# A sigmoid gate in one ScalarE pass, row scales by Newton steps on VectorE, and another order for the last tile

## The chip, the cores and the metric

The kernel runs on one core of a Trainium2 chip. The metric is the device time of one execution in microseconds (us). The kernel before the change took 1693.11 us (median of three runs, 1692.22 to 1693.23). The engines are named as in the profile: PE is TensorE (its matmuls; PEld is its weight loads), ACT is ScalarE, DVE is VectorE, POOL is GpSimd, SP is SyncE, which here only issues DMAs.

## What is computed

One encoder layer over 1280 tokens (1024 of one request, 256 of another) of width 1024, all in f32: an input projection, two kinds of attention, an output projection, a squared-ReLU MLP, and then the part that this document is about, a gated embedding and the final norm:

```python
def _rms_norm(x, g, eps):
    xf = x.astype(jnp.float32)
    y = xf * lax.rsqrt(jnp.mean(xf * xf, axis=-1, keepdims=True) + eps)
    return (y * g.astype(jnp.float32)).astype(x.dtype)

# end of the layer
    gate = jax.nn.sigmoid(jnp.einsum('bsd,de->bse', _rms_norm(h, g_ple, NORM_EPS), w_ple_gate))
    h = h + gate * jnp.einsum('bsp,pd->bsd', p_l, w_ple_proj)
    return h
# after the only layer
    return _rms_norm(h, g_final, NORM_EPS)
```

`h` is 1280 x 1024, `w_ple_gate` is 1024 x 1024, `p_l` is 1280 x 256 and `w_ple_proj` is 256 x 1024.

## The kernel before

Tokens lie in ten tiles of 128 rows. A matrix product in near-f32 precision is made of three products of rounded parts (high times high, high times low, low times high), so that the gate of one tile and one half of the columns is 24 matmuls (8 blocks of 128 rows, three products each) of 512 columns, and the embedding's product is 6. The last stage, from about 1535 us on, is a loop over the ten tiles in the order `FORD`; before it come the last products of the MLP.

For each tile `gate_input` (L1510) transposes the tile on PE (`trg`, 8 matmuls), splits it into its high part on ACT (L1518) and its low part on DVE (L1519), and takes the sum of squares of each row on ACT in two halves (L1523, into `gss`). From that sum `rsqrt` (L135) makes the row scale `rn`: a scale and an offset on DVE (L138), a logarithm and an exponential on ACT (L139, L140), and one correction step on ACT and DVE (L142 to L144). L1527 turns its sign. `gate_input` of a tile is called one turn of the loop ahead, and its transposes stand on PE one further tile ahead.

Then `gate` (L1580) runs the 24 matmuls of a half into a PSUM bank `psg` and makes the sigmoid out of parts: an exponential on ACT (L1592), a limit and plus one on DVE (L1593), a logarithm and an exponential on ACT, which together are the reciprocal (L1594, L1595), and one correction step on POOL and DVE (L1596, L1597). `embed` (L1600) runs the 6 matmuls of the embedding into a bank `psp`. `add` (L1610) multiplies the two on DVE (L1613), subtracts the result from `h` (its sign is turned) on POOL (L1615), and takes the sum of squares of the new rows on ACT (L1616, into `fss`). For the last two tiles (`late`) POOL's two operations are made on DVE.

When both halves are done, `rsqrt` makes the row scale `rf` of the final norm, L1644 multiplies each half by `rf` and the gain `gfin` on DVE, and a DMA of 256 KB on SP's queue writes it to `y` (L1645).

The last tile is cut into three pieces of 512, 256 and 256 columns. Their three gates come first on PE, then the three embeddings. For the two small pieces the gain is multiplied in ahead of the row scale (L1634), so that ACT can finish them (L1639) while DVE finishes the first piece (L1644); the DMAs for the two halves both stand on SP's queue.

The order within each engine is made by a list scheduler from the order in which the code is written and from its own model of durations; `tc.issue_after` adds an edge by hand. All of ACT's functions here (exponential, logarithm, square, copy) are in one table set, loaded once at the start (L115).

Of the kernel before, what the change touches and what calls it, by code (L numbers as in the profile page):

```python
# [14 lines left out]
F32 = mybir.dt.float32  # L15
F32R = mybir.dt.float32r
F16 = mybir.dt.float16
AF = mybir.ActivationFunctionType
ALU = mybir.AluOpType
AX = mybir.AxisListType  # L20
# [3 lines left out]
P = 128  # L24
D = 1024
# [20 lines left out]
def encoder_kernel(ctx: ExitStack, tc: tile.TileContext, x, xT, pT, w_in, w_out, w_ff1, w_ff2, w_gate, w_proj,  # L46
# [88 lines left out]
    def rsqrt(dst, src, scale, eps, tp, n, tag):  # L135
        vv = tp.tile([P, n], F32, tag=f"{tag}v", name=f"{tag}v")
        uu = tp.tile([P, n], F32, tag=f"{tag}u", name=f"{tag}u")
        V.tensor_scalar(vv, src, scale, eps, op0=ALU.mult, op1=ALU.add)  # L138
        S.activation(uu, vv, AF.Ln)  # L139
        S.activation(dst, uu, AF.Exp, scale=-0.5)  # L140
        if n == 1:
            S.activation(uu, dst, AF.Copy, scale=-0.5)  # L142
            V.scalar_tensor_tensor(vv, dst, dst, vv, op0=ALU.mult, op1=ALU.mult)
            V.scalar_tensor_tensor(dst, vv, -3.0, uu, op0=ALU.add, op1=ALU.mult)  # L144
            return
# [3 lines left out]
        V.tensor_tensor(dst, dst, uu, op=ALU.mult)  # L149

    rstd1 = cp.tile([P, NT], F32, name="rstd1")

# [889 lines left out]
    while owed > 0:  # L1042
        d = next(side)
# [466 lines left out]
    def gate_input(t):  # L1510
# [10 lines left out]
        for n in range(2):  # L1521
            jk = gq_.tile([P, 512], F32, tag="gjk", name="gjk", bufs=1)
            S.activation(jk, h_half(t, n), AF.Square, accum_out=ss[:, n:n + 1])  # L1523
        V.tensor_tensor(ss[:, 0:1], ss[:, 0:1], ss[:, 1:2], op=ALU.add)
        rn = gq_.tile([P, 1], F32, tag="grn", name="grn")
        rsqrt(rn, ss[:, 0:1], 1.0 / D, 1e-6, gq_, 1, "grs")
        S.activation(rn, rn, AF.Copy, scale=-1.0)  # L1527
        return n3h, n3l, rn

    QUADS = {2: (0, 0, "H6"), 3: (0, 1, "L2"), 4: (1, 0, "H4"), 5: (1, 1, "L3")}  # L1530
# [27 lines left out]
    for ti, t in enumerate(FORD):  # L1558
# [16 lines left out]
            banks[0].append(pj("psg"))  # L1575
            banks[1].append(bank("tr", "psp"))

        ends = []

        def gate(i):  # L1580
            n0, nn = pieces[i]
            n = slice(n0, n0 + nn)
            ps = banks[0][i][:, :nn]
            pr = []
            for k in range(KD):
                pr += [(n3h[:, k], gw[k][0][:, n]), (n3h[:, k], gw[k][1][:, n]), (n3l[:, k], gw[k][0][:, n])]
            for m, (a, b) in enumerate(pr):
                ends[:] = [PE.matmul(ps, a, b, start=m == 0, stop=m == len(pr) - 1)]  # L1588

            e = gq_.tile([P, 512], F32, tag="ge", name="ge", bufs=3)[:, :nn]  # L1590
            d = gq_.tile([P, 512], F32, tag="gd", name="gd")[:, :nn]
            S.activation(e, ps, AF.Exp, scale=rn)  # L1592
            V.tensor_scalar(d, e, 1e18, 1.0, op0=ALU.min, op1=ALU.add)  # L1593
            S.activation(e, d, AF.Ln)  # L1594
            S.activation(e, e, AF.Exp, scale=-1.0)  # L1595
            (V if late else G).tensor_tensor(d, d, e, op=ALU.mult)  # L1596
            V.scalar_tensor_tensor(e, d, -2.0, e, op0=ALU.add, op1=ALU.mult)  # L1597
            return e

        def embed(i):  # L1600
# [9 lines left out]
        def add(i, e, pq):  # L1610
            n0, nn = pieces[i]
            n = slice(n0, n0 + nn)
            V.tensor_tensor(e, pq, e, op=ALU.mult)  # L1613
            h = h_half(t, n0 // 512)[:, n0 % 512:n0 % 512 + nn]
            (V if late else G).tensor_tensor(h, h, e, op=ALU.subtract)  # L1615
            S.activation(e, h, AF.Square, accum_out=ss[:, i:i + 1])  # L1616
# [12 lines left out]
        i = 2 if last else 1  # L1629
        V.tensor_tensor(ss[:, 0:1], ss[:, 0:1], ss[:, i:i + 1], op=ALU.add)  # L1630
        if last:

            for (n0, nn), e in zip(pieces[1:], es[1:]):
                V.tensor_tensor(e, h_half(t, 1)[:, n0 - 512:n0 - 512 + nn], gfin[:, n0:n0 + nn], op=ALU.mult)  # L1634
        rf = gq_.tile([P, 1], F32, tag="rf", name="rf", bufs=1)
        rsqrt(rf, ss[:, 0:1], 1.0 / D, 1e-6, gq_, 1, "rf")
        if last:
            for (n0, nn), e in zip(pieces[1:], es[1:]):
                S.activation(h_half(t, 1)[:, n0 - 512:n0 - 512 + nn], e, AF.Copy, scale=rf)  # L1639
            dma(y[t * P:(t + 1) * P, 512:], h_half(t, 1))  # L1640
        for n0 in range(0, 512 if last else D, 512):
            n = slice(n0, n0 + 512)
            h = h_half(t, n0 // 512)
            V.scalar_tensor_tensor(h, h, rf, gfin[:, n], op0=ALU.mult, op1=ALU.mult)  # L1644
            dma(y[t * P:(t + 1) * P, n], h)  # L1645


def _rope_tables():
# [48 lines left out]
```

## Time and profile before

| what | us |
|---|---|
| three runs, median | 1693.11 |
| the profiled execution, its own time | 1691.84 |
| its span, first to last instruction | 1690.1 |
| PE busy | 1651.6 (98% of the span) |
| DVE, ACT, POOL busy | 1179.9, 868.0, 661.0 |
| mean granted TensorE clock | 0.997 |

The page's busy times are means over the whole program. The change touches only the last tenth of it, so the views that matter are those of the stretch from 1535 us to the end. In the rows of the timeline the columns are: start in us, length in us, engine, line and operation, what is written `<-` what is read with the shape, how many instructions were merged (`x24`), and in brackets how long the engine had been idle before it and what ended that. A row of the busy-time table by stretches has the stretch, its length, and for each engine the busy time with the number of instructions, then the granted clock, the DMA share and GB/s.

### The profile page before, as it was taken

To read this page: it belongs to the slowest core of one execution; us is meant where nothing else is said; L and a number is where in the kernel's file an instruction comes from. 1 tells how busy PE (TensorE), PEld (TensorE's weight loads), DVE (VectorE), ACT (ScalarE), POOL (GpSimd) and SP (SyncE) were. 2 spreads that over 40 slices of the span, in tenths; PEclk is the share of its full clock that TensorE was granted. 3 is DMA by queue.
4 is the path that set the end of the run, shared out by engine and by line. 5 is a ranking of instruction groups with operands and counts; after the bars stand their busy time and mean duration, and the time that the engine had idled before them with its cause. 6 is when DMAs were issued, how large, how long until landed. Compare 5 with 4: busy or idle time off the path is not lost.

```text
span 1690.1 us, 27269 instructions
## 1 busy us (share of the span) xinstructions
PE 1651.6 (98%) x9849; PEld 1482.7 (88%) x9849; DVE 1179.9 (70%) x2119; ACT 868.0 (51%) x1749; POOL 661.0 (39%) x647
## 2 busy tenths in 40 slices
PE   8999999999899999999999999999999999999997
PEld 8999888888788888889999999998888888888886
DVE  7778588777888888668666666666665855445666
ACT  8643377776766667674333333233433333354554
POOL 1223455555654445433566665620532400001441
PEclk9999999999999999999999999999999999999999
DMA  9766843433954524395443343349676356532111
GB/s 309 239 216 237 247 144 110 133 108 98 273 161 130 154 74 131 108 330 172 160 136 131 132 159 128 135 169 386 220 225 203 124 192 210 177 117 75 35 44 50
DMA packets 191867, 278.28 MB, mean 165 GB/s; under 512 B 13674, under 2 KB 121076, under 8 KB 191732
## 3 DMA queue, kind: packets, MB, share of 16 engines
q1 hardware_dynamic: 189988, 271.28, 49.7%
q0 software_dynamic: 1600, 5.24, 1.0%
q8 instruction: 78, 1.28, 0.3%
q14 instruction: 57, 0.47, 0.1%
q10 hardware_dynamic: 144, 0.00, 0.0%
HBM read 182.63 MB, written 88.61 MB: 160 GB/s over the span
## 4 chain that ended last, share of the span: by engine, by line
PE 79%; DVE 8%; ACT 4%; issue 4%; POOL 2%; DMA 2%; POOLq 0%; SPq 0%; ACTq 0%; DVEq 0%
PE psa L264 6%; PE sc L651 6%; PE av L729 5%; PE psb L264 4%; PE pso L264 4%; PE tr L705 4%; PE psv L264 2%; PE psg L1588 1%; DVE pl L716 1%; DVE p L686 1%; DMA xt<-in_x 1%; POOL hq L1615 1%; DMA xr<-in_xT 1%; PE f__15605 L156 1%; PE f__16642 L156 1%
## 5 line engine op out<-in xcount | busy, mean ns | idle before, releaser
L1384 ACT ACTIVATE ao<-ar 128x1280 fp32r<-128x1280 f32 x56 | 71.2, 1273 | 183.7 <-PE f__15946 L156 36.6
L651 PE MATMUL sc<-kt,qt 128*128 128x512 f32 (+1 forms) x576 | 156.6, 392 | 8.8 <-ACT p L676 6.1
L716 DVE TENSOR_TENSOR pl<-tr,ph 128x512 fp32r<-128x512 f32 x204 | 138.0, 685 | 32.0 <-ACT ph L711 30.8
L1386 DVE TENSOR_TENSOR ao<-ar,ao 128x1280 fp32r<-128x1280 f32 x56 | 93.3, 1666 | 85.2 <-ACT ao L1384 85.2
L711 ACT ACTIVATE ph<-tr 128x512 fp32r<-128x512 f32 x204 | 120.0, 596 | 59.2 <-PE tr L705 52.7
L651 PEld LDWEIGHTS sc<-kt,qt 128*128 128x128 f32 x576 | 98.8, 189 | 27.1 <-ACT p L676 7.6
L264 PE MATMUL pso<-ow,mt 128*128 128x512 f32 x480 | 119.9, 396 | 2.0 <-DVE osq L756 1.3
L705 PE MATMUL tr<-ident,p 128*128 128x128 f32 x768 | 116.0, 274 | 5.8 <-DVE pl L716 5.1
L1588 PE MATMUL psg<-gw,n 128*128 128x512 f32 (+1 forms) x504 | 113.7, 381 | 0.0
L705 PEld LDWEIGHTS tr<-ident,p 128*128 128x128 f32 x768 | 91.6, 141 | 22.6 <-DVE pl L716 9.0
L1105 POOL TENSOR_SCALAR w1r<-w1r,gmlp 128x256 f32<-128x256 f32 x112 | 80.3, 735 | 68.4 <-DMA w1r<-in_w_ff 68.4
L1588 PEld LDWEIGHTS psg<-gw,n 128*128 128x128 f32 x504 | 90.9, 188 | 17.8
L264 PEld LDWEIGHTS pso<-ow,mt 128*128 128x128 f32 x480 | 88.0, 189 | 19.9 <-DVE osq L756 2.0
L729 PE MATMUL av<-ph,vt 128*128 128x256 f32 x544 | 101.8, 288 | 1.0 <-ACT ph L711 0.4
L690 POOL TENSOR_SCALAR p<-p,rl 128x1024 f32<-128x1024 f32 x64 | 76.2, 1192 | 50.6 <-DVE rl L688 49.1
L1178 ACT ACTIVATE w<-w1s 128x512 fp32r<-128x512 f32 x56 | 35.2, 629 | 114.7 <-POOL w1s L1185 55.3
L668 DVE TENSOR_REDUCE mm<-sc 128x1 f32<-128x1024 f32 (+1 forms) x80 | 84.2, 1056 | 9.4 <-PE sc L651 9.0
L729 PE MATMUL av<-pl,vt 128*128 128x256 f32 x408 | 89.4, 300 | 0.0
L729 PEld LDWEIGHTS av<-ph,vt 128*128 128x128 f32 x544 | 81.8, 188 | 6.4 <-DVE osq L756 0.8
L676 ACT ACTIVATE p<-sc,mm 128x1024 f32<-128x1024 f32 x64 | 71.4, 1116 | 25.1 <-DVE mm L668 16.3
L664 DVE CUSTOM_DVE_ANT_0 p<-sc,dist 128x1024 f32<-128x1024 f32 x64 | 77.6, 1218 | 7.8 <-PE sc L651 3.8
L673 ACT ACTIVATE p<-p,mm 128x1024 f32<-128x1024 f32 x64 | 73.5, 1149 | 18.0 <-DVE mm L664 17.2
(1520 smaller groups left out, 4705.9 us busy)
## 6 DMA issues: line engine op xcount, KB each, us to landing
ar<-ad SPq DMA_DIRECT2D x56, 640.0 KB, 4.0
w2r<-in_w_ff SPq DMA_DIRECT2D x56, 512.0 KB, 4.6
qt<-qd SPq DMA_DIRECT2D x160, 128.0 KB, 3.0
ad<-q SPq DMA_DIRECT2D x64, 320.0 KB, 2.8
ad<-qs SPq DMA_DIRECT2D x48, 320.0 KB, 2.2
w1r<-in_w_ff SPq DMA_DIRECT2D x28, 512.0 KB, 4.3
md<-ml SPq DMA_DIRECT2D x40, 256.0 KB, 2.5
mt<-md SPq DMA_DIRECT2D x20, 512.0 KB, 5.7
```

Of the source, the lines that this page charges most:

```text
L264: PE.matmul(ps, a, b, start=i == 0, stop=i == n - 1)
L651: PE.matmul(ps[:, h0:h0 + n], shared["q"][:, cc, v, i * P:(i + 1) * P], kt[:, s0 + h0:s0 + h0 + n], start=v == 0, stop=v == 1)
L664: V.tensor_tensor_reduce(out=p[:, :sn], in0=ps[:, :sn], in1=dst_t[:, off:off + sn], scale=SLOPES[idx], scalar=3.0e38, op0=ALU.add, op1=ALU ...
L668: V.tensor_reduce(out=st["m", i][:, 0:1], in_=ps[:, :sn], axis=AX.X, op=ALU.max, negate=True)
L690: G.tensor_scalar(p[:, :sn], p[:, :sn], rl[:, 0:1], 1.0, op0=ALU.mult, op1=ALU.mult)
L705: PE.transpose(t[:, jj, i * P:(i + 1) * P], st["ws"][i][:, j * P:(j + 1) * P], ident)
L711: S.activation(ph, st["tr", j2], AF.Copy)
L716: V.tensor_tensor(pl, st["tr", j2], f(st["ph", j2][:]), op=ALU.subtract)
L729: PE.matmul(st["av"][:, :256], x_, y_, start=j2 == 0 and n == 0, stop=j2 == nj - 1 and n == len(pr) - 1)
L1105: G.tensor_scalar(raw[:, k], raw[:, k], gmlp[:, 4 * kh + k:4 * kh + k + 1], 1.0, op0=ALU.mult, op1=ALU.mult)
L1386: V.tensor_tensor(ao[:, 1], a, f(ao[:, 0]), op=ALU.subtract)
L1588: ends[:] = [PE.matmul(ps, a, b, start=m == 0, stop=m == len(pr) - 1)]
```

## The change

Three things are edited.

The gate becomes one ACT pass, `Sigmoid` of the PSUM bank times the row scale (L1609 of the new text); the six operations that made it out of parts are gone, and the product is added to `h` and not subtracted. Sigmoid is in another table set, so a load stands ahead of the first one; the last tile loads the former set again by hand, behind its last sigmoid, for the logarithm and exponential of the final `rsqrt`.

The row scales of all tiles but the last one's final norm come from `rsqrt_d`: a first guess out of the number's bits and three Newton steps, nine small DVE operations of 128x1 in all (L158 to L165), none on ACT.

In the last tile the first piece's embedding is put ahead of the third piece's gate on PE; the sums of squares are written into a buffer of their own; the sum of the first two pieces is scaled before the third one's is there; the gain is multiplied into all three pieces ahead of the row scale; and the second half's DMA is issued on ACT's queue, while the first half's stays on SP's.

```diff
+    def rsqrt_d(dst, ss, tp, n, tag, eng=V, bufs=None, rest=None):
+        vv = tp.tile([P, n], F32, tag=f"{tag}v", name=f"{tag}v", bufs=bufs)
+        uu = tp.tile([P, n], F32, tag=f"{tag}u", name=f"{tag}u", bufs=bufs)
+        c = -0.5e-6
+        if rest is not None:
+            eng.tensor_scalar(uu, rest, -0.5 / D, c, op0=ALU.mult, op1=ALU.add)
+            c = uu
+        eng.tensor_scalar(vv, ss, -0.5 / D, c, op0=ALU.mult, op1=ALU.add)
+        eng.tensor_scalar(dst.bitcast(I32), vv[:].bitcast(I32), -0.5, float(0x5F3759DF - 2**30 - 2**22), op0=ALU.mult, op1=ALU.add)
+        for _ in range(3):
+            if n == 1:
+                eng.tensor_scalar(uu, dst, dst, vv, op0=ALU.mult, op1=ALU.mult)
+                eng.tensor_scalar(dst, uu, 1.5, dst, op0=ALU.add, op1=ALU.mult)
...
-        V.tensor_tensor(ss[:, 0:1], ss[:, 0:1], ss[:, 1:2], op=ALU.add)
         rn = gq_.tile([P, 1], F32, tag="grn", name="grn")
-        rsqrt(rn, ss[:, 0:1], 1.0 / D, 1e-6, gq_, 1, "grs")
-        S.activation(rn, rn, AF.Copy, scale=-1.0)
+        rsqrt_d(rn[:], ss[:, 1:2], gq_, 1, "grs", rest=ss[:, 0:1])
...
-            S.activation(e, ps, AF.Exp, scale=rn)
-            V.tensor_scalar(d, e, 1e18, 1.0, op0=ALU.min, op1=ALU.add)
-            S.activation(e, d, AF.Ln)
-            S.activation(e, e, AF.Exp, scale=-1.0)
-            (V if late else G).tensor_tensor(d, d, e, op=ALU.mult)
-            V.scalar_tensor_tensor(e, d, -2.0, e, op0=ALU.add, op1=ALU.mult)
+            sig[:] = [S.activation(e, ps, AF.Sigmoid, scale=rn)]
...
-            (V if late else G).tensor_tensor(h, h, e, op=ALU.subtract)
+            (V if late else G).tensor_tensor(h, h, e, op=ALU.add)
+            if last:
+                e = gq_.tile([P, 512], F32, tag="gjk", name="gjk", bufs=1)[:, :nn]
             S.activation(e, h, AF.Square, accum_out=ss[:, i:i + 1])
 
         if last:
-            es = [gate(i) for i in range(3)]
-            with tc.issue_after(ends[0].ins):
-                qs = [embed(i) for i in range(3)]
+            es = [gate(i) for i in range(2)]
             for i in range(3):
-                add(i, es[i], qs[i])
+                if i == 1:
+                    es.append(gate(2))
+                    with tc.issue_after(sig[0].ins):
+                        S.preload_act_table_set("natural_log_exp_and_others")
+                with tc.issue_after(ends[0].ins):
+                    pq = embed(i)
+                add(i, es[i], pq)
                 if i == 1:
                     V.tensor_tensor(ss[:, 0:1], ss[:, 0:1], ss[:, 1:2], op=ALU.add)
+                    V.tensor_scalar(ss[:, 0:1], ss[:, 0:1], 1.0 / D, 1e-6, op0=ALU.mult, op1=ALU.add)
...
+            premult(0)
+            first = rsqrt(rf, ss[:, 2:3], 1.0 / D, ss[:, 0:1], gq_, 1, "rf")
+            with tc.issue_after(first.ins):
+                premult(1)
+                premult(2)
+        else:
+            rsqrt_d(rf[:], ss[:, i:i + 1], gq_, 1, "rf", rest=ss[:, 0:1])
         if last:
+            V.tensor_scalar(h_half(t, 0), es[0], rf, None, op0=ALU.mult)
+            dma(y[t * P:(t + 1) * P, :512], h_half(t, 0))
             for (n0, nn), e in zip(pieces[1:], es[1:]):
                 S.activation(h_half(t, 1)[:, n0 - 512:n0 - 512 + nn], e, AF.Copy, scale=rf)
-            dma(y[t * P:(t + 1) * P, 512:], h_half(t, 1))
...
+            S.dma_start(y[t * P:(t + 1) * P, 512:], h_half(t, 1))
```

The instructions of each engine stand in the same order as before up to the last products of the MLP, among which the first row scales of the gate are made. Three places show what moves at the end of the program. The first is ACT at the end of the last tile, before (`psg` is the gate's bank, `ge` and `gd` are its scratch, `fss` the sums of squares):

```order
L1592 ACTIVATE ge<-psg,grn 128x256
L1594 ACTIVATE ge<-gd 128x256
L1595 ACTIVATE ge<-ge 128x256
L1592 ACTIVATE ge<-psg,grn 128x256
L1594 ACTIVATE ge<-gd 128x256
L1595 ACTIVATE ge<-ge 128x256
L1616 ACTIVATE ge,fss<-hq 128x512
L1616 ACTIVATE ge,fss<-hq 128x256 x2
L139 ACTIVATE rfu<-rfv 128x1
L140 ACTIVATE rf<-rfu 128x1
L142 ACTIVATE rfu<-rf 128x1
L1639 ACTIVATE hq<-ge,rf 128x256 x2
```

and with the change:

```order
L1609 ACTIVATE ge<-psg,grn 128x512
L1609 ACTIVATE ge<-psg,grn 128x256
L1630 ACTIVATE gjk,fss<-hq 128x512
L1609 ACTIVATE ge<-psg,grn 128x256
L1638 ACT_TABLE_LOAD
L1630 ACTIVATE gjk,fss<-hq 128x256 x2
L140 ACTIVATE rfu<-rfv 128x1
L141 ACTIVATE rf<-rfu 128x1
L143 ACTIVATE rfu<-rf 128x1
L1666 ACTIVATE hq<-ge,rf 128x256 x2
L1667 DMA y<-hq 128x512
```

One pass per piece is left of three, the first piece's square (L1630) now stands ahead of the last piece's sigmoid, a table load stands between that sigmoid and the last two squares, and ACT issues a DMA at its end.

The second place is DVE in the last tile (its rows before stand in the same stretch as L1593, L1596, L1597, L1613 and L1615 of three pieces, interleaved). With the change, from the first piece's product on:

```order
L1625 TENSOR_TENSOR ge<-psp,ge 128x512
L1627 TENSOR_TENSOR hq<-hq,ge 128x512
L1651 TENSOR_TENSOR ge<-hq,gfin 128x512
L1625 TENSOR_TENSOR ge<-psp,ge 128x256
L1627 TENSOR_TENSOR hq<-hq,ge 128x256
L1625 TENSOR_TENSOR ge<-psp,ge 128x256
L1627 TENSOR_TENSOR hq<-hq,ge 128x256
L1643 TENSOR_TENSOR fss<-fss 128x1
L1644 TENSOR_SCALAR fss<-fss 128x1
L139 TENSOR_SCALAR rfv<-fss 128x1
L1651 TENSOR_TENSOR ge<-hq,gfin 128x256 x2
L144 SCALAR_TENSOR_TENSOR rfv<-rf,rfv 128x1
```

Per piece the product, the sum and (for the first) the gain are left; the gains of the two small pieces (L1651) have moved behind the first operation of the row scale (L139).

The third place is PE in the last tile, before:

```order
L1588 MATMUL psg<-gw,n_18106 128x256 x48
L156 MATMUL psp<-pw,p_h 128x512 x2
L156 MATMUL psp<-pw,p_l 128x512
L156 MATMUL psp<-pw,p_h 128x512 x2
L156 MATMUL psp<-pw,p_l 128x512
L156 MATMUL psp<-pw,p_h 128x256 x2
```

and with the change (the other 24 matmuls of 128x256, the second piece's gate, stand ahead of these rows):

```order
L176 MATMUL psp<-pw,p_h 128x512 x2
L176 MATMUL psp<-pw,p_l 128x512
L176 MATMUL psp<-pw,p_h 128x512 x2
L176 MATMUL psp<-pw,p_l 128x512
L1606 MATMUL psg<-gw,n_18035 128x256 x24
L176 MATMUL psp<-pw,p_h 128x256 x2
```

The first piece's six embedding matmuls have moved ahead of the third piece's gate; the matmuls are the same in number and shape.

More of the change, by code (lines that the diff above doesn't have):

```diff
@@ L17 @@
 F16 = mybir.dt.float16
+I32 = mybir.dt.int32
 AF = mybir.ActivationFunctionType
@@ L137, in rsqrt @@
         uu = tp.tile([P, n], F32, tag=f"{tag}u", name=f"{tag}u")
-        V.tensor_scalar(vv, src, scale, eps, op0=ALU.mult, op1=ALU.add)
+        first = V.tensor_scalar(vv, src, scale, eps, op0=ALU.mult, op1=ALU.add)
         S.activation(uu, vv, AF.Ln)
@@ L144, in rsqrt @@
             V.scalar_tensor_tensor(dst, vv, -3.0, uu, op0=ALU.add, op1=ALU.mult)
-            return
+            return first
         V.tensor_tensor(uu, dst, dst, op=ALU.mult)
@@ L149, in rsqrt @@
         V.tensor_tensor(dst, dst, uu, op=ALU.mult)
+    def rsqrt_d(dst, ss, tp, n, tag, eng=V, bufs=None, rest=None):
[12 more added lines that the diff above has]
+            else:
+                eng.tensor_tensor(uu, dst, dst, op=ALU.mult)
+                eng.tensor_tensor(uu, uu, vv, op=ALU.mult)
+                eng.scalar_tensor_tensor(dst, uu, 1.5, dst, op0=ALU.add, op1=ALU.mult)
     rstd1 = cp.tile([P, NT], F32, name="rstd1")
@@ L1576, in encoder_kernel @@
             banks[1].append(bank("tr", "psp"))
-        ends = []
+        ends, sig = [], []
         def gate(i):
@@ L1590, in gate @@
             e = gq_.tile([P, 512], F32, tag="ge", name="ge", bufs=3)[:, :nn]
-            d = gq_.tile([P, 512], F32, tag="gd", name="gd")[:, :nn]
-            S.activation(e, ps, AF.Exp, scale=rn)
-            V.tensor_scalar(d, e, 1e18, 1.0, op0=ALU.min, op1=ALU.add)
-            S.activation(e, d, AF.Ln)
-            S.activation(e, e, AF.Exp, scale=-1.0)
-            (V if late else G).tensor_tensor(d, d, e, op=ALU.mult)
-            V.scalar_tensor_tensor(e, d, -2.0, e, op0=ALU.add, op1=ALU.mult)
+            sig[:] = [S.activation(e, ps, AF.Sigmoid, scale=rn)]
             return e
@@ L1629, in encoder_kernel, with premult @@
         i = 2 if last else 1
-        V.tensor_tensor(ss[:, 0:1], ss[:, 0:1], ss[:, i:i + 1], op=ALU.add)
+        def premult(i):
+            n0, nn = pieces[i]
+            V.tensor_tensor(es[i], h_half(t, n0 // 512)[:, n0 % 512:n0 % 512 + nn], gfin[:, n0:n0 + nn], op=ALU.mult)
+        rf = gq_.tile([P, 1], F32, tag="rf", name="rf", bufs=1)
         if last:
[L1633 to L1636, printed above, removed]
+            premult(0)
[3 more added lines that the diff above has]
+                premult(2)
+        else:
+            rsqrt_d(rf[:], ss[:, i:i + 1], gq_, 1, "rf", rest=ss[:, 0:1])
         if last:
+            V.tensor_scalar(h_half(t, 0), es[0], rf, None, op0=ALU.mult)
+            dma(y[t * P:(t + 1) * P, :512], h_half(t, 0))
             for (n0, nn), e in zip(pieces[1:], es[1:]):
                 S.activation(h_half(t, 1)[:, n0 - 512:n0 - 512 + nn], e, AF.Copy, scale=rf)
[L1640 to L1645, printed above, removed]
+            S.dma_start(y[t * P:(t + 1) * P, 512:], h_half(t, 1))
+        else:
+            for n in range(2):
+                h = h_half(t, n)
+                V.scalar_tensor_tensor(h, h, rf, gfin[:, n * 512:n * 512 + 512], op0=ALU.mult, op1=ALU.mult)
+                dma(y[t * P:(t + 1) * P, n * 512:n * 512 + 512], h)
 def _rope_tables():
```

## The prediction

> **What bounds the kernel now.** The page's first part gives PE nearly all of the span:
>
> ```profile
> PE 1651.6 (98%) x9849; PEld 1482.7 (88%) x9849; DVE 1179.9 (70%) x2119; ACT 868.0 (51%) x1749; POOL 661.0 (39%) x647
> ```
>
> A mean says nothing about one stage, so I read next the busy time by stretches: the stage of the gate up to the end of its last matmul, and what is left behind it.
>
> ```profile
> 1535.00:1679.08 144.08, 144.08 (x695) 120.70 (x693) 90.09 (x165) 73.57 (x196) 48.77 (x40) 1.00 0.12 43
> 1679.08:1690.10 11.02, 0.00 (x0) 0.00 (x0) 5.86 (x18) 4.04 (x13) 0.00 (x0) 0.66 0.13 48
> ```
>
> In the first row PE is busy for all of the 144.08 us, at full clock; ACT, DVE and POOL have half of it or less. Passes taken off these three there bring nothing unless PE waits for one of them, and it doesn't. In the second row PE has no instruction for 11.02 us. This is the only stretch in which the change can gain, so the third view is the timeline of the last tile. PE first:
>
> ```profile
> 1664.91 11.36 PE L1588 MATMUL psg<-gw,n 128*128 128x512 f32 x72
> 1676.10 0.63 PE L156 MATMUL psp<-pw,p_h 128*128 128x512 f32 x2
> 1677.49 0.40 PE L156 MATMUL psp<-pw,p_h 128*128 128x256 f32 x2
> 1678.08 0.28 PE L156 MATMUL psp<-pw,p_l 128*128 128x256 f32 x1
> 1678.80 0.28 PE L156 MATMUL psp<-pw,p_l 128*128 128x256 f32 x1
> ```
>
> The three gates are issued from 1664.91 to 1676.10, the first piece's embedding up to 1677.49, the second one's last matmul ends at 1678.36 and the third one's at 1679.08. Then ACT, DVE and SP's queue:
>
> ```profile
> 1678.24 0.46 ACT L1592 ACTIVATE ge<-psg,grn 128x256 f32<-128x256 f32 x1
> 1682.33 0.42 DVE L1613 TENSOR_TENSOR ge<-psp,ge 128x256 f32<-128x256 f32 x1
> 1682.79 0.42 DVE L1615 TENSOR_TENSOR hq<-hq,ge 128x256 f32<-128x256 f32 x1
> 1683.24 0.42 ACT L1616 ACTIVATE ge<-hq 128x256 f32<-128x256 f32 x1 [0.29 <-DVE hq L1615]
> 1683.79 0.16 DVE L1630 TENSOR_TENSOR fss<-fss 128x1 f32<-128x1 f32 x1 [0.17 <-ACT ge L1616]
> 1683.87 0.42 DVE L1634 TENSOR_TENSOR ge<-hq,gfin 128x256 f32<-128x256 f32 x1
> 1684.20 0.15 DVE L138 TENSOR_SCALAR rfv<-fss 128x1 f32<-128x1 f32 x1
> 1684.38 0.20 ACT L139 ACTIVATE rfu<-rfv 128x1 f32<-128x1 f32 x1 [0.63 <-DVE rfv L138]
> 1684.62 0.20 ACT L140 ACTIVATE rf<-rfu 128x1 f32<-128x1 f32 x1
> 1684.85 0.22 DVE L143 SCALAR_TENSOR_TENSOR rfv<-rf,rfv 128x1 f32<-128x1 f32 x1 [0.51 <-ACT rf L140]
> 1685.18 0.16 DVE L144 SCALAR_TENSOR_TENSOR rf<-rfv,rfu 128x1 f32<-128x1 f32 x1
> 1685.37 0.91 ACT L1639 ACTIVATE hq<-ge,rf 128x256 f32<-128x256 f32 x2 [0.32 <-DVE rf L144]
> 1685.37 0.75 DVE L1644 SCALAR_TENSOR_TENSOR hq<-hq,rf,gfin 128x512 f32<-128x512 f32 x1
> 1686.15 0.33 SPq L1645 DMA_DIRECT2D y<-hq  x1
> 1686.58 0.46 SPq L1640 DMA_DIRECT2D y<-hq  x1
> ```
>
> The last embedding is there at 1679.08, but its product (L1613) starts only at 1682.33: the third piece's exponential runs at 1678.24, and its five further passes go to and fro between the engines. From there on it is one chain: sum, square, row scale, scaling of the output, DMA. The last DMA starts at 1686.58, and the span ends 3.52 us later.
>
> **The change, part by part, against the span of 1690.1 us.** Steps from one start to the next are read off the rows above: 0.46 from a product of 256 columns to its sum (1682.33 to 1682.79), 0.45 on to the square, 0.55 on to DVE's next small operation, 0.18 from there to the logarithm, 0.24 to the exponential, 0.23 back to DVE, 0.33 to the second correction, 0.19 to the scaling. DVE can issue the next independent operation of 256 columns 0.33 after the last (1683.87 to 1684.20), and 0.08 after a small one (1683.79 to 1683.87).
>
> *PE in the last tile.* The same matmuls in another order: its end stays at 1679.08. A gate of 512 columns takes 5.44 (from 1658.11 to the embedding at 1663.55, rows below), so the two small gates share 11.19 - 5.44 = 5.75, 2.87 each. The first piece's embedding (1.39, from 1676.10 to 1677.49) now comes ahead of the third gate, whose issue ends at 1677.49 and whose result is there 0.17 later, as above (1664.91 + 11.36 against 1676.10). The first piece's product, sum, gain and square then run from about 1674.8 to 1676.9, under the third gate; if that cover were gone they would cost the chain some 2 us.
>
> *The gate in one pass.* The third sigmoid starts at 1677.70, 0.04 behind its bank (as ACT does at 1649.21, below, behind 1643.57 + 5.60), and takes the 0.46 of the exponential's row, since it reads the same bank by the same scale. Its own price is not in the trace; between a row of 0.42 (another pass of 256 columns) and the exponential's 0.69 for 512 columns (below) it changes nothing, by the slack below.
>
> *The table load.* It stands on ACT between this sigmoid and the last two squares. The only load that the trace has is the one at the start:
>
> ```profile
> 0.74 1.28 ACT L115 ACT_TABLE_LOAD   x1 [0.74 <-PEq L1688]
> ```
>
> With 1.28 it runs from 1678.16 to 1679.44. The second piece's product can start at 1678.40 (0.04 behind its last matmul), its sum at 1678.86, its square at 1679.31, with the load at 1679.44. The third piece's product follows on DVE at 1679.20, its sum at 1679.66, its square at 1680.11. The second square is over on ACT by 1679.87, so the load has 0.24 us to spare: at a price from 0 to 1.52 it costs nothing. Twice the row, 2.57, is my upper bound; the squares then start at 1680.73 and 1681.16, and all behind them moves by 1.05. I take 1.28, the row of the same instruction.
>
> The Trainium skill (ScalarE: Activation LUTs, What ACT_TABLE_LOAD costs) puts a switch to another set at 1283 ns for the load plus a drain of about 1380 ns, 2.66 us in all; its first part agrees with the row, the second no row here shows, since nothing ran ahead of that load. By it the sum would end 1.14 us later.
>
> The load ahead of the first sigmoid has cover: ACT waits long enough for the first gate to end.
>
> ```profile
> 1542.89 0.69 ACT L1592 ACTIVATE ge<-psg,grn 128x512 f32<-128x512 f32 x1 [7.14 <-PE psg L1588]
> ```
>
> *The row scale of the last tile.* L139 of the new text starts 0.55 behind the last square, at 1680.66, with no sum of halves ahead of it. Logarithm 1680.84, exponential 1681.08, back on DVE at 1681.31; there the two moved gains (1680.74 and 1681.08) hold the queue until about 1681.42. Corrections at 1681.42 and 1681.75, scaling on ACT at 1681.94, for 0.91 as now: 1682.85. DVE's part of the scaling (one pass of 512 columns with one scalar, 0.43 by L1593 below) lies beside it.
>
> *The DMAs.* Now SP is held by its first DMA, and the second starts 0.30 behind ACT's end (1686.28 to 1686.58). With ACT's own queue I take 0.03, the distance of L1644's end from SP's DMA: 1682.88. Landing is bounded by these two rows, SP's outputs in the last 31 us and the one DMA that ACT issues now, small and at a cold start:
>
> ```profile
> y<-hq SPq DMA_DIRECT2D x8, 256.0 KB, 2.0
> gmix<-in_g_mix ACTq DMA_DIRECT2D x1, 4.0 KB, 2.8
> ```
>
> I take 2.0, the row of the same transfer, and keep 0.8 more for the range.
>
> *The sum.* Last square 1683.24 to 1680.11: -3.13. Square to scaling, 2.13 to 1.83: -0.30. Scaling to last DMA, 1.21 to 0.94: -0.27. Together -3.70, and the span becomes 1686.4.
>
> *The other nine tiles.* A tile takes PE 14.54 us (the second gates of two neighbouring tiles start at 1643.57 and 1658.11):
>
> ```profile
> 1643.57 5.60 PE L1588 MATMUL psg<-gw,n 128*128 128x512 f32 x24
> 1649.21 0.69 ACT L1592 ACTIVATE ge<-psg,grn 128x512 f32<-128x512 f32 x1 [0.59 <-PE psg L1588]
> 1656.51 1.29 DVE L1519 TENSOR_TENSOR n<-trg,n 128x512 fp32r<-128x512 f32 x2 [1.15 <-ACT n L1518]
> 1658.11 5.60 PE L1588 MATMUL psg<-gw,n 128*128 128x512 f32 x24
> 1663.55 0.62 PE L156 MATMUL psp<-pw,p_h 128*128 128x512 f32 x2
> L1615 POOL TENSOR_TENSOR hq<-hq,ge 128x512 f32<-128x512 f32 x16 | 22.4, 1400 | 36.3 <-DVE ge L1613 36.3
> L1644 DVE SCALAR_TENSOR_TENSOR hq<-hq,rf,gfin 128x512 f32<-128x512 f32 x19 | 13.5, 748 | 0.3
> L1613 DVE TENSOR_TENSOR ge<-psp,ge 128x512 f32<-128x512 f32 x19 | 13.1, 691 | 1.2
> L143 DVE SCALAR_TENSOR_TENSOR grsv<-grn,grsv 128x1 f32<-128x1 f32 x8 | 10.0, 1251 | 0.0
> L1593 DVE TENSOR_SCALAR gd<-ge 128x512 f32<-128x512 f32 x19 | 8.2, 432 | 7.3 <-ACT ge L1592 7.3
> L1569 POOL TENSOR_TENSOR p_l<-pr,p_h 128x256 fp32r<-128x256 f32 x8 | 5.9, 742 | 2.4 <-ACT p_h L1568 2.4
> L138 DVE TENSOR_SCALAR rfv<-fss 128x1 f32<-128x1 f32 x10 | 1.5, 153 | 0.3
> ```
>
> DVE keeps six large passes per tile (two products, two low parts of the transposed tile, two outputs: 4 x 0.69 + 2 x 0.75 = 4.26) and gets 18 small operations for two row scales, at 0.2 each (0.153 by L138 and a hand-over of 0.04): 3.6. That is 7.9 of 14.54. The new wait is that of the final row scale's first operation for a tile's first square; behind it in DVE's queue stand that tile's second product and the low part of a tile two gates ahead. Even now, with the longer chain, the last tile's low part is done at 1657.80 and needed at 1664.91: 7.1 us of cover. So I cost the small operations at nothing; without that cover they are 3.6 a tile.
>
> **How the numbers follow for the runs.** The profiled execution took 1691.84, and would take 1688.1; the runs' median lies 1.27 higher, and so does the forecast: 1693.11 - 3.70 = 1689.4.
>
> **The rivals.** *A: the load is the end's new wait.* It costs the doubled row or more, and the squares wait for ACT: gain 2.65, 1690.5. For it speaks that the load is the one thing on ACT there which no row prices in the midst of work; against it, that 0.24 is spare and the row is 1.28. By the Trainium skill's 2.66 (the section named above) it would be 1690.6.
>
> *B: the DMA from ACT's queue lands later*, by the 0.8 between the rows: gain 2.9, 1690.2. Against it: the 2.8 belongs to a first transfer in tiny packets.
>
> *C: the end does not move,* because something at the stage's head or a re-ordered matmul gives it back; 1693.1. PE's unbroken 144.08 us speak against it.
>
> *D: slower; DVE becomes the bound of the nine tiles.* A 128x1 operation takes 1251 ns in the row of L143, where it ran beside POOL. From 0.57 us each, (14.54 - 4.26) / 18, DVE needs longer than PE for a tile. If all 18 took 1.25, a tile would be 26.8 and eight tiles some 98 us longer, 1791. Against it: POOL keeps two sums and one difference, 2 x 1.40 + 0.74 = 3.54 a tile, and cannot hold DVE for longer than it runs: 4.26 + 3.6 + 3.54 = 11.4, under 14.54.
>
> **Chances.** Forecast 0.60, A 0.20, B 0.11, C 0.05, D 0.04. The range is 1688.5 to 1691.4: below, 0.9 for a chain with shorter hand-overs and the scatter of the runs (1.0 between the three); above, A and B together (1693.11 - 3.70 + 1.05 + 0.8 = 1691.3). What a measurement of this kernel can tell from no change is about 0.2%, 3.4 us, so the forecast lies only just beyond it: of its 0.60 I count 0.50 as faster, and 0.02 of B. Faster 0.52, same 0.43, slower 0.05.
>
> **What would show it.** PE without a gap up to about 1679.1, and no matmul behind it. The second load at about 1678.2, 1.28 long, with the first small square right behind it: right; an idle ACT around it, or squares from 1680.7 on: A. The last square at 1680.1, scaling at 1681.9, ACT's DMA at 1682.9, and 3.5 us from there to the end (4.3: B). DVE's small operations near 0.2 us, and POOL waiting for DVE, not DVE for POOL. Wrong would be all of it if PE showed waits between 1535 and 1679, or if the last DMA started as forecast and the end came no earlier.

## The result, and the profile after

The changed kernel takes 1688.02 us in the median of 11 runs (1686.18 to 1691.33), the kernel before 1692.04 (11 runs, 1688.64 to 1694.14, among them the three from which the forecast started). The ratio is 0.998, with a 95% interval of 0.9971 to 0.9990: faster by 0.2%, which is 4.0 us. The change is small, but the interval leaves out 1.

The profiled span fell from 1690.1 to 1685.6 us, by 4.5. Two measures take this apart, and they serve in all experiments below: the *stage*, from the first matmul of the gate to the end of the last matmul of all, and the *tail*, from there to the end of the span. Busy time by stretches, after the change; the columns are the stretch, its length, then busy time of PE, weight load, DVE, ACT and POOL (with instructions), granted clock, DMA share and GB/s:

```profile
1534.02:1678.14 144.12, 144.12 (x695) 120.75 (x693) 70.46 (x212) 48.66 (x105) 26.27 (x24) 1.00 0.12 43
1678.14:1685.60 7.46, 0.00 (x0) 0.00 (x0) 2.92 (x11) 2.97 (x10) 0.00 (x0) 0.80 0.19 70
```

The stage is 144.12 us, as it was (1534.96 to 1679.08), although DVE, ACT and POOL lost 20 to 25 us of work each. The tail went from 11.02 to 7.46: 3.56 us of the 4.5. The other 0.94 lies ahead of the stage, where both kernels issue the same instructions but for the first row scales. The start of the stage lay between 1532.1 and 1537.2 in the profiled executions of all these kernels, so single times say little of 1 us, and the experiments are read by their tails. A tail rests on a span that is given to 0.1 us, so tails less than 0.1 apart are read as equal.

The timeline of the last tile after the change (start, duration, engine, line, operation; in brackets the idle time ahead of it and what ended it):

```profile
1673.93 0.69 DVE L1625 TENSOR_TENSOR ge<-psp,ge 128x512 f32<-128x512 f32 x1 [3.96 <-PE psp L176]
1676.80 0.47 ACT L1609 ACTIVATE ge<-psg,grn 128x256 f32<-128x256 f32 x1 [0.69 <-PE psg L1606]
1677.29 1.28 ACT L1638 ACT_TABLE_LOAD   x1
1677.86 0.28 PE L176 MATMUL psp<-pw,p_l 128*128 128x256 f32 x1
1678.33 0.42 DVE L1625 TENSOR_TENSOR ge<-psp,ge 128x256 f32<-128x256 f32 x1
1678.59 0.42 ACT L1630 ACTIVATE gjk<-hq 128x256 f32<-128x256 f32 x1
1678.78 0.43 DVE L1627 TENSOR_TENSOR hq<-hq,ge 128x256 f32<-128x256 f32 x1
1679.13 0.16 DVE L1643 TENSOR_TENSOR fss<-fss 128x1 f32<-128x1 f32 x1
1679.30 0.42 ACT L1630 ACTIVATE gjk<-hq 128x256 f32<-128x256 f32 x1 [0.21 <-DVE fss L1643]
1679.84 0.21 DVE L139 TENSOR_SCALAR rfv<-fss 128x1 f32<-128x1 f32 x1 [0.37 <-ACT gjk L1630]
1681.16 0.91 ACT L1666 ACTIVATE hq<-ge,rf 128x256 f32<-128x256 f32 x2 [0.40 <-DVE rf L145]
1681.16 0.49 DVE L1663 TENSOR_SCALAR hq<-ge,rf 128x512 f32<-128x512 f32 x1
1681.67 0.33 SPq L1664 DMA_DIRECT2D y<-hq  x1
1682.10 0.35 ACTq L1667 DMA_DIRECT2D y<-hq  x1
```

The load starts 0.02 behind the third sigmoid's end, and the second square follows 0.02 behind the load. DVE is free when the first piece's embedding comes: its product waited 3.96 us for PE. The last DMA starts at 1682.10, 3.50 us ahead of the end (3.52 before).

| from the end of the last matmul, us | before | forecast | after |
|---|---|---|---|
| last square starts | 4.16 | 1.03 | 1.16 |
| scaling starts | 6.29 | 2.86 | 3.02 |
| last DMA starts | 7.50 | 3.80 | 3.96 |
| end of the span (the tail) | 11.02 | 7.32 | 7.46 |

One thing in the two traces the prediction did not look for: how late DVE is with a tile. The first row of each pair is PE's first embedding of a tile (its first gate has just ended), the second is DVE's first output of the same tile; tiles two and eight, before:

```profile
1554.97 0.62 PE L156 MATMUL psp<-pw,p_h 128*128 128x512 f32 x2
1575.19 1.41 DVE L1644 SCALAR_TENSOR_TENSOR hq<-hq,rf,gfin 128x512 f32<-128x512 f32 x2
...
1642.21 0.62 PE L156 MATMUL psp<-pw,p_h 128*128 128x512 f32 x2
1666.05 1.40 DVE L1644 SCALAR_TENSOR_TENSOR hq<-hq,rf,gfin 128x512 f32<-128x512 f32 x2
```

and after:

```profile
1554.03 0.61 PE L176 MATMUL psp<-pw,p_h 128*128 128x512 f32 x2
1567.68 1.41 DVE L1671 SCALAR_TENSOR_TENSOR hq<-hq,rf,gfin 128x512 f32<-128x512 f32 x2
...
1641.27 0.62 PE L176 MATMUL psp<-pw,p_h 128*128 128x512 f32 x2
1654.90 1.41 DVE L1671 SCALAR_TENSOR_TENSOR hq<-hq,rf,gfin 128x512 f32<-128x512 f32 x2
```

Call the distance the lag. Before, it grows from 20.2 us to 23.8 over six tiles: PE gives out a tile every 14.54 us, the outputs follow every (1666.05 - 1575.19) / 6 = 15.14 in the mean, though unevenly (14.31 to 16.03 from one tile to the next). After, it is 13.65 and 13.63: the outputs keep PE's step. PE never waits in either kernel, so no view of PE shows the difference.

### The profile page after: what moved, and what is told of

Its sections match the earlier page's. It is cut to its first block, busy times and chain, and to the rows that moved or that the text cites. A ratio compares the mean times of both kernels' runs of the same rounds, so it can differ in the third digit from the quotient of the medians.

```text
span 1685.6 us, 27175 instructions
## 1 busy us (share of the span) xinstructions
PE 1650.2 (98%) x9849; PEld 1481.2 (88%) x9849; DVE 1159.4 (69%) x2168; ACT 841.6 (50%) x1642; POOL 637.9 (38%) x631
## 3 DMA queue, kind: packets, MB, share of 16 engines
q8 instruction: 78, 1.28, 0.3%
## 4 chain that ended last, share of the span: by engine, by line
PE 85%; DVE 5%; DMA 3%; issue 2%; ACT 2%; POOL 1%; SPq 1%; ACTq 0%; DVEq 0%; POOLq 0%
PE psg L1606 7%; PE psa L284 6%; PE sc L671 5%; PE pso L284 5%; PE av L749 5%; PE tr L725 4%; PE psb L284 3%; PE psv L284 2%; PE psp L176 2%; DVE pl L736 1%; PE f__15605 L176 1%; DVE mm L688 1%; DMA xr<-in_xT 1%; PE f__16642 L176 1%; PE f__14552 L176 1%
## 5 line engine op out<-in xcount | busy, mean ns | idle before, releaser
L1587 POOL TENSOR_TENSOR p_l<-pr,p_h 128x256 fp32r<-128x256 f32 x10 | 7.4, 742 | 213.8 <-ACT p_h L1586 213.8
```

## The experiments

The theory at the start was the prediction's: all of the gain is made in the last tile, by a shorter chain, and the first nine tiles give nothing. The tails:

| kernel | tail, us |
|---|---|
| before | 11.02 |
| changed | 7.46 |
| nine tiles changed, last tile as before (mid_only) | 8.88 |
| eight tiles changed, last two as before (eight_only) | 8.90 |
| seven tiles changed, last three as before (seven_only) | 8.83 |
| before, eighth tile's POOL passes on DVE (late3) | 9.43 |
| last tile alone changed (last_only) | 8.64 |
| changed, a second load (two_loads) | 8.53 |
| changed, no load by hand (no_preload) | 9.69 |
| changed, PE's old order (embed_last) | 8.35 |
| changed, last DMA on SP (dma_sp) | 7.41 |
| changed, last row scale by Newton (newton_end) | 8.43 |
| changed, second embedding earlier (embed1_early) | 7.41 |
| that, and the last square on DVE (dve_square) | 7.14 |

The stage is 144.11 or 144.12 in every one of them. All kernels of the table below the second row ran once, except dve_square. Their single times would mislead: mid_only took 1689.37 us beside 1689.41 for the kernel before, although its tail is 2.14 shorter.

**The two halves of the change.** mid_only keeps the old last tile behind nine changed ones; last_only is the reverse. The core of each edit, against the changed kernel (where the lines are left out, the exponential and its five passes follow as in the kernel before, for the last tile in mid_only and for the first nine in last_only):

```diff
 # mid_only
-            sig[:] = [S.activation(e, ps, AF.Sigmoid, scale=rn)]
+            if not last:
+                sig[:] = [S.activation(e, ps, AF.Sigmoid, scale=rn)]
+                return e
...
 # last_only
+            if last:
+                sig[:] = [S.activation(e, ps, AF.Sigmoid, scale=rn)]
+                return e
...
```

> The first nine tiles are changed, the last tile is as before (gate in parts, its old order and end; the former table set is loaded behind the ninth tile's last sigmoid). 'Tail' is the stretch from the end of the last matmul to the end of the span: 11.02 us before, 7.46 us with the whole change. Theory 1 (one chain through the engines' queues, work of the ninth tile included): the ninth tile leaves ACT and DVE earlier, the last tile's first pass starts at its bank (some 3 us earlier than before), its passes run under the gates, and DVE's products, sums and the third piece's last correction then decide: last square 2.1 earlier, tail 8.9. Theory 2 (only the last tile's own passes count, as the prediction had it): tail 11.0. The stage from the first gate matmul to the last matmul: 144.1 as before under both; a rival that the nine tiles hold PE up would have it shorter.

> The first nine tiles are as before (gate in parts, row scales through ACT; only the ninth tile's final row scale is by Newton steps, so that no logarithm falls between the sigmoids), the last tile is changed. Theory 1: the ninth tile's passes still hold DVE until some 1.8 us ahead of the last matmul's end, the last tile's products queue behind them, and the first square, behind which the third sigmoid and the load stand on ACT, is late: tail 8.8. Theory 2: tail 7.5, the whole gain.

mid_only has a tail of 8.88: 2.14 us come from the nine tiles alone. last_only has 8.64: 2.38 from the last tile alone. Together they would be 4.52, and the change brings 3.56, so the two shares overlap. The 2.38 is not exact either: in last_only the ninth tile's final row scale is by Newton steps and takes 2.11 us up to the output (1670.81 to 1672.92), where the kernel before takes 1.44 (1673.77 to 1675.21); without that the share could be up to some 0.7 larger. last_only shows where the nine tiles enter:

```profile
1672.92 1.42 DVE L1687 SCALAR_TENSOR_TENSOR hq<-hq,rf,gfin 128x512 f32<-128x512 f32 x2
1674.25 0.68 DVE L1637 TENSOR_TENSOR ge<-psp,ge 128x512 f32<-128x512 f32 x1
1676.33 0.46 ACT L1613 ACTIVATE ge<-psg,grn 128x256 f32<-128x256 f32 x1
1676.80 1.28 ACT L1650 ACT_TABLE_LOAD   x1
```

The ninth tile's output (L1687) holds DVE until 1674.34, and the last tile's first product starts as it ends, 2.01 ahead of the last matmul's end (1676.26), where the changed kernel has it 4.21 ahead (1673.93 against 1678.14). So the first square comes late, and behind it on ACT the third sigmoid and the load, which now set the squares. That the nine tiles bring nothing has fallen.

**How far back the lag comes from.** The next theory was that the ninth tile's passes stand in the last tile's way. eight_only and seven_only move the border of mid_only forward by one tile and by two (the row scales of the normalization stay Newton's):

```diff
-            if not last:
+            if ti < NT - 2:      # eight_only;  seven_only: NT - 3
                 sig[:] = [S.activation(e, ps, AF.Sigmoid, scale=rn)]
```

> The first eight tiles of the gate as changed (sigmoid, both row scales by Newton steps), the ninth and the tenth as before (exponential with its five further passes, final row scale by logarithm and exponential, table load by hand behind the eighth tile's last sigmoid; only the row scales of these two tiles' normalization, made tiles earlier, are Newton's). It differs from the kernel with nine changed tiles in the ninth tile alone. Theory (the ninth tile's passes stand in the last tile's way, those of the first eight in nobody's): the tail goes back to 10.8 to 11.0 us, and the last tile's first exponential starts some 5.4 us ahead of the last matmul's end, as before. Rival (passes saved in all nine tiles build up a lead that the last tile lives on): the tail stays near 8.9, the first exponential some 8.5 us ahead. The stage from the first gate to the last matmul is 144.1 in either case.

The tail is 8.90 and the last tile's first exponential starts 8.53 us ahead of the last matmul's end: the rival's numbers, and my theory fell. One old tile in front takes nothing back.

> As the kernel with eight changed tiles, but the eighth tile too in the old form (its two passes of the gate and sums on POOL included); seven tiles changed, the last three as before. Theory, formed after the run with eight changed tiles: in the kernel before ACT and DVE run late behind PE (the eighth tile's last output is made at 1666.05, 16.9 us behind the end of its last gate, where the kernel with eight changed tiles has 6.6), because a tile's chain goes through POOL and waits in the queues behind the tile ahead of it; the lag is one tile's own, so one old tile in front of the last two brings it back: the eighth tile's output 13 to 17 us behind its gate, and a tail of 10 to 11 us. Rival (the lead grows over many tiles): the eighth tile's output stays under 12 us behind its gate and the tail at 8.9 to 9.5. The stage stays at 144.1 in either case.

The eighth tile's output comes 12.4 us behind its second gate's end (1662.89 against 1650.46), a little over the rival's bound, but the tail is 8.83, and the theory fell again:

```profile
1671.84 0.69 ACT L1620 ACTIVATE ge<-psg,grn 128x512 f32<-128x512 f32 x1 [0.59 <-PE psg L1612]
```

In seven_only the last tile's first exponential waits for PE, as it should. In the kernel before it stood behind other work on ACT:

```profile
1673.64 0.67 ACT L1592 ACTIVATE ge<-psg,grn 128x512 f32<-128x512 f32 x1
```

That is 5.44 ahead of the last matmul's end, 3.1 later than in seven_only. Two old tiles in front of the last one are caught up again. The lag tells what is a tile's own and what is built up: the first old tile of seven_only has 19.39 us (1662.89 against PE's first embedding at 1643.50) behind changed tiles with 13.6, so some 5.8 are the longer chain of one old tile, while the same tile of the kernel before has 23.84. That the other 4.45 grow tile by tile is read off the kernel before itself (20.2 at tile two); seven_only leaves the row scales of the normalization to Newton's steps, so it doesn't show what their old form in the last tiles costs. The next run asks what in an old tile makes the loss. late3 is the kernel before with one number changed:

```diff
-        late = ti >= NT - 2
+        late = ti >= NT - 3
```

> The kernel before with one number changed: its last three tiles, not its last two, have the gate's product and the sum on DVE where the others have them on POOL. All passes are kept, the exponential form too; only the eighth tile leaves POOL. Theory (the lag of the eighth tile comes from the passes on POOL, 1.3 to 1.4 us each against 0.69 on DVE, and from DVE's small operations that POOL holds up for 1.25): the eighth tile's output comes 2 us or more earlier behind its gate than the 16.9 of the kernel before, and the tail falls from 11.0 to 9 to 10. Rival (the number of passes per tile makes the lag, wherever they run): DVE only gets more work, the eighth tile's output stays at about 17 us and the tail at 11.0 or above.

The tail is 9.43, as the theory had it, with all passes kept:

```profile
1648.67 0.21 DVE L143 SCALAR_TENSOR_TENSOR rfv<-rf,rfv 128x1 f32<-128x1 f32 x1
1660.78 1.42 DVE L1644 SCALAR_TENSOR_TENSOR hq<-hq,rf,gfin 128x512 f32<-128x512 f32 x2
1671.81 0.67 ACT L1592 ACTIVATE ge<-psg,grn 128x512 f32<-128x512 f32 x1
```

The eighth tile's output comes 11.8 behind its gate's end (1648.96) in place of 16.9, and the last tile's first exponential 7.06 ahead of the last matmul's end: 1.62 earlier than before, for a tail that is 1.59 shorter. The first of the rows is a small correction that in the kernel before ran beside a POOL pass:

```profile
1648.41 1.32 DVE L143 SCALAR_TENSOR_TENSOR rfv<-rf,rfv 128x1 f32<-128x1 f32 x1 [0.93 <-ACT rf L140]
1648.42 1.29 POOL L1596 TENSOR_TENSOR gd<-gd,ge 128x512 f32<-128x512 f32 x1 [2.07 <-ACT rf L140]
```

It ends with POOL's pass. The Trainium skill (SBUF — State Buffer, SBUF: two separate sides) says that VectorE with two inputs from SBUF and GpSimd take a shared port in turn, for a whole instruction; 1.32 beside POOL against 0.21 without agrees. This correction belongs to the seventh tile, whose output came no sooner in late3 (1650.20 against 1650.03, in a stage that began 0.20 earlier), so it is an example of the hold and not what moved the eighth tile. The kernel before points the same way: its ninth tile, the first that makes its passes on DVE, is back at a lag of 18.5 (1675.21 against 1656.75). Shown is that taking one tile's passes off POOL shortens the tail by 1.6 us, where changing nine tiles shortens it by 2.1. What part of this comes from the longer passes on POOL, from the operations that POOL holds up, or from the number of passes, was not measured apart.

**The table load.** two_loads puts a second, useless load ahead of the one by hand; no_preload takes the one by hand away, so that the compiler places them.

```diff
 # two_loads
                     with tc.issue_after(sig[0].ins):
+                        one = S.preload_act_table_set("sigmoid_and_others")
+                    with tc.issue_after(one.ins):
                         S.preload_act_table_set("natural_log_exp_and_others")
 # no_preload
-                    with tc.issue_after(sig[0].ins):
-                        S.preload_act_table_set("natural_log_exp_and_others")
```

> The changed kernel with a second, useless table load ahead of the one in the last tile. If a load is 1.28 us and the one in the trace ended just as its square became ready, the last square starts 1.0 later (a second load of 1.28 less the slack that the last square had behind the first small one): tail 8.5. If ACT's load is off the chain altogether: 7.5. If a switch costs a drain beside the load, 2.66 by the Trainium skill (ScalarE: Activation LUTs, What ACT_TABLE_LOAD costs): 9.8.

```profile
1678.03 0.47 ACT L1609 ACTIVATE ge<-psg,grn 128x256 f32<-128x256 f32 x1 [0.69 <-PE psg L1606]
1678.52 1.28 ACT L1638 ACT_TABLE_LOAD   x1
1679.81 1.28 ACT L1640 ACT_TABLE_LOAD   x1
1681.11 0.42 ACT L1630 ACTIVATE gjk<-hq 128x256 f32<-128x256 f32 x1
```

A load takes 1.28 in the midst of work too, and the next instruction starts 0.01 to 0.02 behind it. The tail grew by 1.07, which is 1.28 less the 0.21 for which ACT was idle ahead of the last square: the slack of the prediction was 0.24. The drain of about 1.38 us that the Trainium skill (ScalarE: Activation LUTs, What ACT_TABLE_LOAD costs) adds to each switch does not show; with 2.66 the tail would have grown by some 2.4.

> The changed kernel without the load by hand: the compiler puts a load ahead of the final logarithm and another ahead of the exponential behind it. Both stand in the chain: the exponential starts at about 1682.6 in place of 1680.33, tail 7.46 + 2.3 = 9.7. If each switch cost 2.66: 12.4.

```profile
1682.99 1.28 ACT L140 ACT_TABLE_LOAD   x1
1684.29 0.20 ACT L140 ACTIVATE rfu<-rfv 128x1 f32<-128x1 f32 x1
1684.51 1.28 ACT L141 ACT_TABLE_LOAD   x1
1685.80 0.20 ACT L141 ACTIVATE rf<-rfu 128x1 f32<-128x1 f32 x1
```

Without the load by hand there are two, one ahead of the logarithm and one ahead of the exponential, both on the chain: the tail is 9.69, 2.23 longer. The one line that places the load is worth 2.23 of the tail's 3.56 us.

**PE's order, the DMA's queue, the row scale.** embed_last puts the three gates ahead of the three embeddings again, dma_sp issues the last DMA from SP, newton_end makes the last row scale by `rsqrt_d`, drops the load and has the two small gains ahead of the row scale; of each edit the core:

```diff
 # embed_last
-            es = [gate(i) for i in range(2)]
+            es = [gate(i) for i in range(3)]
 # dma_sp
-            S.dma_start(y[t * P:(t + 1) * P, 512:], h_half(t, 1))
+            dma(y[t * P:(t + 1) * P, 512:], h_half(t, 1))
 # newton_end
-            first = rsqrt(rf, ss[:, 2:3], 1.0 / D, ss[:, 0:1], gq_, 1, "rf")
+            rsqrt_d(rf[:], ss[:, 2:3], gq_, 1, "rf", rest=ss[:, 0:1])
```

> The changed kernel with the last tile's old order on PE: three gates, then three embeddings. The prediction said that without its cover the first piece would cost the chain some 2 us (tail 9.5). Worked out from the durations of the changed kernel's trace, with the scheduler's order on DVE (first product, second product, first sum, second sum, third product, first gain, third sum): the third sum starts at 1679.7 in place of 1678.8, tail 7.46 + 0.85 = 8.3. If the order on PE does not matter: 7.5.

The tail is 8.35, longer by 0.89. The prediction had 2 us for a lost cover; what the chain pays is less, because the first piece's square on ACT (1679.00) runs beside the products and sums that DVE still has to make (the third product at 1679.22); the last square starts 2.12 behind the last matmul in place of 1.16.

> The changed kernel with its last DMA on SP's queue again, behind the first half's. The prediction gave ACT's queue 0.27 us: tail 7.75. By the changed kernel's trace SP is free at 1682.00 and ACT's scaling ends at 1682.07, so that SP no longer holds it up: tail 7.5.

```profile
1680.71 0.91 ACT L1666 ACTIVATE hq<-ge,rf 128x256 f32<-128x256 f32 x2 [0.40 <-DVE rf L145]
1681.65 0.38 SPq L1667 DMA_DIRECT2D y<-hq  x1
```

The tail is 7.41, no longer than with ACT's queue. SP's second DMA starts 0.03 behind the scaling's end: its first one is issued at 1681.23 and no longer in the way. What freed SP is DVE's pass of 0.49 (L1663 of the changed kernel) in the place of one of 0.75 (L1644 of the kernel before).

> The changed kernel with the last tile's final row scale by Newton steps too, without any table load at the end. In the trace the steps take 2.12 us from their first operation to the scaling (1666.44 to 1668.56) where the chain through ACT takes 1.32 (1679.84 to 1681.16); one gain now stands ahead of the last sum on DVE (0.2): tail 7.46 + 1.0 = 8.5. If the load is what delays the end, 0.1 to 0.2 of it come back: 8.3.

The tail is 8.43, longer by 0.97: eight small operations on DVE take 2.1 us (1681.79 to 1683.90; the ninth, L158, runs ahead of them, while the last sum of squares is still being made) where the way over ACT took 1.3. Without the load they start no earlier: 1.92 behind the last matmul's end, against 1.70 in the changed kernel.

**What is left of the load.** embed1_early puts the second piece's embedding ahead of the third gate too:

```diff
-                if i == 1:
+                if i == 2:
                     es.append(gate(2))
```

> The changed kernel with the second piece's embedding ahead of the third gate as well. DVE is then free when the last embedding ends, and the last sum starts 0.15 earlier; but the third sigmoid ends 0.7 later on ACT and the load with it, at 1679.27 in the times of the changed kernel, where the last square would be ready at 1679.15. If the load is the next wait: tail 7.45, no gain. If it is not in the way: 7.3.

```profile
1677.90 1.28 ACT L1638 ACT_TABLE_LOAD   x1
1679.19 0.42 ACT L1630 ACTIVATE gjk<-hq 128x256 f32<-128x256 f32 x1
```

The tail is 7.41. The last square starts at 1679.19 and the load ends at 1679.18 (1677.90 + 1.28). So the load is the next wait, as expected, but not by the earlier sums alone: behind the third gate that now ends later, the load itself ends 1.10 behind the last matmul (1678.08) in place of 0.43. dve_square keeps this order and takes the load off the chain; the core of the edit:

```diff
+            if last and i == 2:
+                V.tensor_tensor_reduce(out=e, in0=h, in1=h, scale=1.0, scalar=0.0,
+                                       op0=ALU.mult, op1=ALU.add, accum_out=ss[:, i:i + 1])
+            else:
                 S.activation(e, h, AF.Square, accum_out=ss[:, i:i + 1])
```

> The changed kernel with the second piece's embedding, too, ahead of the third gate, the first two pieces' gains right behind their sums, and the third piece's square on DVE (product with itself and its row sum in one instruction) where ACT made it behind the table load. Theory (the table load sets the start of the last square, and nothing else does): the last sum ends some 0.98 us behind the last matmul and the square follows at once on DVE, 0.45 long, so that the sum of squares is there at 1.45 where the changed kernel has it at 1.58 (last square 1.16 behind the last matmul, 0.42 long), and the load is off the chain; with the hand-over from ACT to DVE gone as well the tail is some 7.1 us. Rival (the load only covers the chain of DVE, and a reduction on DVE is dearer than one on ACT): the square takes 0.6 or more and the tail is 7.4 to 7.5 as in the changed kernel. The stage from the first gate to the last matmul stays at 144.1. Against the kernel before the time is some 0.998 in either case, since 0.3 us are below what the runs can tell.

```profile
1678.47 1.28 ACT L1641 ACT_TABLE_LOAD   x1
1679.22 0.42 DVE L1627 TENSOR_TENSOR hq<-hq,ge 128x256 f32<-128x256 f32 x1
1679.68 0.43 DVE L1631 CUSTOM_DVE_ANT_0 gjk<-hq 128x256 f32<-128x256 f32 x1
1680.04 0.08 DVE L1631 DVE_READ_ACCUMULATOR2_ANT fss<- 128x1 f32 x1
1680.16 0.21 DVE L139 TENSOR_SCALAR rfv<-fss 128x1 f32<-128x1 f32 x1
```

The tail is 7.14, as the theory had it: the row scale starts 1.50 behind the last matmul's end (1678.66) in place of 1.70, and with one gain fewer behind its first operation it is 0.09 shorter on DVE (1680.16 to the first correction at 1680.87, before that 1679.84 to 1680.64). In time the kernel takes 1688.13 in the median of 11 runs, against 1691.27 (15 runs) for the kernel before; ratio 0.9982, interval 0.9973 to 0.9991. Its tail is the shortest of all, but against the changed kernel its time cannot be told apart.

## Why the prediction was right, and where it was wrong

- *The time.* Forecast 1689.4 in a range of 1688.5 to 1691.4, measured 1688.02: as a time it lies 0.48 below the range. The kernel before was itself 1.07 lower over 11 runs than over the three of the forecast (1692.04 against 1693.11). As a gain the forecast was 3.70, in a range of 1.7 to 4.6, and 4.02 was measured. The range took the scatter from three runs that lay 1.0 apart; the 11 runs of each kernel lie more than 5 us apart.
- *The sum for the tail.* -3.70 forecast, -3.56 measured, term by term: last square -3.00 for -3.13, square to scaling -0.27 for -0.30, scaling to DMA -0.27 for -0.27, and 0.02 from the DMA to the end. The 0.13 of the first is in two places, 0.07 each: the third piece's product came later behind its last matmul (0.19 for 0.12), and the last square waited, by its row, for L1643, a small sum that DVE makes in between.
- *"Passes taken off these three there bring nothing unless PE waits for one of them, and it doesn't"* is the step that failed: mid_only shows 2.14 us from the first nine tiles, with a PE that never waits. It was argued from PE: no gap, so nothing to gain. But the sum for the last tile has the first product at about 1674.8, which supposes a DVE that is free, and in the kernel before it is not. The prediction took the nine tiles' share without naming it. By last_only, the last tile's edits alone give 2.38. That the sum still came out is luck: the nine tiles put at nothing and a DVE taken as free are two mistakes that cancelled in the number, not in the reasoning. The rows of L1644 in the trace were there to see the lag grow.
- *The load* cost 1.28 and had 0.21 to spare (forecast 0.24). Rival A, a dearer load as the next wait, fell by two_loads and no_preload. Its place was right: the slack is so small that in embed1_early, where the load came 0.67 later and the sums earlier, it was the next wait.
- *The embedding as cover* was mis-sized: 0.9 by embed_last, not 2.
- *ACT's own DMA queue* was right in its number and wrong in its cause: the 0.27 came by the shorter pass on DVE, and dma_sp has it too. Rival B fell: 3.50 us from the last DMA to the end.
- *DVE's small operations* were put at 0.2. In the groups of the changed kernel a Newton step's first half, with two row scalars, takes 0.27:

```profile
L164 DVE TENSOR_SCALAR rfu<-rf,rfv 128x1 f32<-128x1 f32 x27 | 7.4, 273 | 0.8
L165 DVE TENSOR_SCALAR rf<-rfu,rf 128x1 f32<-128x1 f32 x27 | 5.8, 214 | 1.0
L161 DVE TENSOR_SCALAR rf<-rfv 128x1 int32<-128x1 int32 x9 | 1.4, 154 | 0.1
```

  Eight of the nine take 2.12 (1666.44 to 1668.56 in the ninth tile). They cost nothing, as forecast: the lag stays at 13.6. Rival D, with operations of 1.25 beside POOL, did not come, and not for want of overlap:

```profile
1636.10 1.30 POOL L1627 TENSOR_TENSOR hq<-hq,ge 128x512 f32<-128x512 f32 x1
1636.76 0.20 DVE L165 TENSOR_SCALAR grn<-grsu,grn 128x1 f32<-128x1 f32 x1
```

  In the gate's stage of the kernel before, 22 operations of 128x1 on DVE take 0.58 to 1.32 us, and each ends within 0.02 of the end of a POOL pass. All of them read two tensors (`SCALAR_TENSOR_TENSOR`, `TENSOR_TENSOR`). In the changed kernel 16 Newton operations run wholly inside a POOL pass and take 0.20 to 0.21 each; they are `TENSOR_SCALAR`, with one tensor and one row scalar. So the prediction priced rival D by an operation of another form. No run changed the form alone.
- *Rival C*, an end that does not move, fell with the tail. The load ahead of the first sigmoid lay under the first gate, as forecast.

## What to carry to other kernels

An engine without a gap does not prove that the work behind it is free: compare, for several rounds, when the bounding engine hands a piece over and when its last result is made; where that distance grows, as it did here before the change, the followers are slower than the leader and the bill comes at the end. Cost the last round with the queues as the rounds before leave them, not with empty ones. A table load belongs on the engine behind the last use of the old set, where one line decided over 2.2 us here.

## What the runs showed that was not expected

- Followers with 62% busy time at most can be too slow for their leader. Busy time of eight tiles before the change, in the columns used above:

```profile
1539.00:1655.00 116.00, 116.00 (x545) 96.42 (x544) 72.33 (x127) 60.47 (x163) 45.33 (x37) 1.00 0.11 39
```

  DVE works for 72.33 of 116 us, ACT for 60.47, POOL for 45.33, and the outputs still take 15.14 us a tile against PE's 14.54.
- A table load is 1.28 us at every place where these kernels have one (at the start, under the first gate, between two tiles, at the end, two in a row). Where nothing else holds the instruction behind it, as in two_loads and no_preload, it starts 0.01 to 0.02 later.
- A row sum on DVE is not dearer than on ACT: 0.43 and 0.08 for the read-out of the sum (dve_square), where ACT takes 0.42 and 0.19.
